# Two DMA rings that cut a batch into windows: equal transfers of 32 KB packets, and thirteen staged batches in place of twelve

## The chip, the cores and the metric

The kernel runs on one core of a Trainium2 chip. Its time is the device time of one execution in microseconds, and the figure that counts is the median over several runs. One more execution was recorded by the hardware profiler, and everything said about stages comes from that execution.

## What is computed

The input `x` has 32 batches of 4096 rows of 256 floats, 4 MiB a batch. The output holds, for each batch, 127 windows of 64 rows, each starting 32 rows after the one before:

```python
for i in range(n_windows):            # (4096 - 64) // 32 + 1 = 127
    start = i * stride                # stride 32, window_size 64
    result[:, i] = x[:, start:start + window_size].copy()
```

There is no arithmetic. With a block of 32 rows (32 KB, 128 blocks to a batch) as the unit, window w consists of blocks w and w+1. A window is 64 KB, and a batch of the output is 127 x 64 KB. Each block but a batch's first and last goes to two places: the second half of one window and the first half of the next.

## The kernel before

All work is done by DMA. Two engines issue it, SyncE (SP) and ScalarE (ACT), and each fills a ring of its own on the core's 16 DMA engines. In the profile SP's ring is q1 and ACT's is q10. A batch takes one of two ways.

**Copied batches** (20, on SP's ring). The windows are copied from HBM to HBM, 127 rows of 64 KB. `copy` makes three transfers of a batch, by `COPY_PARTS`: 80 rows with each row in 4 packets of 16 KB, 32 rows in 2 packets of 32 KB, and 15 rows in 4 packets of 16 KB. The first two are dealt out to 16 DMA engines and the third to 15, so that 15 engines carry 5 + 2 + 1 = 8 rows of a batch and one carries 7.

**Staged batches** (12, the odd ones from 1 to 23, in `STAGED`; on ACT's ring). `load` brings the 128 blocks to one of five SBUF tiles, a block to a partition. `store` writes the tile twice, once to the first halves of the windows and once to the second halves, 128 blocks each time. Each of the three transfers has 16 KB packets (`2 * BLOCK_PARTS` parts of 64 KB), so 16 packets to a DMA engine. ACT issues load n+1 before it waits for load n and issues the two stores of n. The 128th block of a store doesn't belong to the batch: one store runs over into the first half window of the batch above, the other into the last half window of the batch below. What stands there has to be written again.

**The order** (`_order`). A batch beside a staged one is therefore copied after its neighbours' stores have landed, which SP waits for (`after_store`, line 73). Four such batches, `EARLY`, are copied first of all; ACT waits for them (`early`) before the first store that touches them, and at the end SP writes their spoilt half windows again with small transfers of 16 packets of 2 KB (`half`, called the mends here; 7 of them). The other copies are placed in SP's program by a formula that puts each some way behind the stage that it depends on. SP issues all copies one after another with no other waits; the ring itself holds it back when it is full. Last, SP waits for everything and clears the semaphores, one instruction for each.

Of the kernel before, what the change touches and what calls it, by code (L numbers as in the profile page):

```python
# [1 line left out]

# [4 lines left out]


STAGED = tuple(range(1, 24, 2))
BUFS = 5  # L10

EARLY = (18, 20, 22, 24)

BLOCK_PARTS = 2

COPY_PARTS = ((80, 4), (32, 2), (15, 4))


class _Geometry:


    def __init__(self, x, out, W, S):
        self.B, self.L, self.D = x.shape
        self.x, self.out = x, out
        self.n_win = (self.L - W) // S + 1
        self.n_blk = self.L // S
        self.blk = S * self.D
        self.win = W * self.D
        assert W == 2 * S and self.n_blk == self.n_win + 1 == 128

    def src(self, b, block, dims):

        at = (b * self.n_blk + block) * self.blk
        return bass.AP(self.x.tensor, self.x.offset + at, dims)

    def dst(self, b, half, dims):

        at = b * self.n_win * self.win + half * self.blk
        return bass.AP(self.out.tensor, self.out.offset + at, dims)

    def rows(self, b, w0, n):

        s, d = [[self.blk, n], [1, self.win]], [[self.win, n], [1, self.win]]
        return self.dst(b, 2 * w0, d), self.src(b, w0, s)

    def half(self, b, half, block):

        dims = [[self.blk // 16, 16], [1, self.blk // 16]]
        return self.dst(b, half, dims), self.src(b, block, dims)


class _Kernel:
    def __init__(self, nc, g, tiles):
        self.nc, self.g, self.tiles = nc, g, tiles
        self.loaded = [nc.alloc_semaphore(f"loaded{i}") for i in range(len(tiles))]
        self.stored = [nc.alloc_semaphore(f"stored{i}") for i in range(len(tiles))]
        self.copied = nc.alloc_semaphore("copied")
        self.early = nc.alloc_semaphore("early")
        self.count = {}

    def start(self, engine, out, in_, sem, parts=1):
        engine.dma_start(out=out, in_=in_, max_dma_last_dim=65536 // parts).then_inc(sem, 16)
        self.count[id(sem)] = self.count.get(id(sem), 0) + 16

    def all_of(self, engine, sem):
        engine.wait_ge(sem, self.count[id(sem)])

    def slot(self, n):
        return divmod(n, len(self.tiles))

    def after_store(self, engine, n):
        turn, i = self.slot(n)
        engine.wait_ge(self.stored[i], 32 * (turn + 1))

    def load(self, n):

        g, (_, i) = self.g, self.slot(n)
        if n >= len(self.tiles):
            self.after_store(self.nc.scalar, n - len(self.tiles))
        src = g.src(STAGED[n], 0, [[g.blk, g.n_blk], [1, g.blk]])  # L80
        self.start(self.nc.scalar, self.tiles[i][:, :], src, self.loaded[i], 2 * BLOCK_PARTS)

    def store(self, n):

        g, (turn, i) = self.g, self.slot(n)
        self.nc.scalar.wait_ge(self.loaded[i], 16 * (turn + 1))
        for half in (0, -1):
            dst = g.dst(STAGED[n], half, [[g.win, g.n_blk], [1, g.blk]])  # L90
            self.start(self.nc.scalar, dst, self.tiles[i][:, :], self.stored[i], 2 * BLOCK_PARTS)

    def copy(self, b, sem):

        w = 0
        for rows, parts in COPY_PARTS:
            self.start(self.nc.sync, *self.g.rows(b, w, rows), sem, parts)
            w += rows
        assert w == self.g.n_win


def _order(B):


    near = {b for s in STAGED for b in (s - 1, s + 1)}
    order = list(EARLY) + [b for b in range(B) if b not in near and b not in STAGED]
    tied = sorted(near - set(EARLY))
    n = len(order) + len(tied)
    for b in tied:
        behind = max(STAGED.index(s) for s in (b - 1, b + 1) if s in STAGED)  # L110
        order.insert(-(-(2 * behind + 5) * n // (2 * len(STAGED))), b)
    return order


@with_exitstack
def kernel(
    ctx: ExitStack,
    tc: tile.TileContext,
    x: bass.AP,
    window_size: bass.AP,  # L120
    stride: bass.AP,
    out: bass.AP,
):
    nc = tc.nc
    W, S = int(window_size), int(stride)
    g = _Geometry(x, out, W, S)
    assert 0 not in STAGED and g.B - 1 not in STAGED
    pool = ctx.enter_context(tc.tile_pool(name="blocks", bufs=1))
    tiles = [pool.tile([g.n_blk, g.blk], x.dtype, name=f"xb{i}") for i in range(BUFS)]

    with tc.tile_critical():
        k = _Kernel(nc, g, tiles)
        for b in _order(g.B):
            if b not in EARLY:
                for s in (b - 1, b + 1):
                    if s in STAGED:
                        k.after_store(nc.sync, STAGED.index(s))
            k.copy(b, k.early if b in EARLY else k.copied)
        k.load(0)
        waited = False  # L140
        last = len(STAGED) - 1
        for n, s in enumerate(STAGED):
            if n < last:
                k.load(n + 1)
            if not waited and (s - 1 in EARLY or s + 1 in EARLY):
                k.all_of(nc.scalar, k.early)
                waited = True
            k.store(n)


        k.all_of(nc.sync, k.early)
        for n, s in enumerate(STAGED):
            if s - 1 in EARLY or s + 1 in EARLY:
                k.after_store(nc.sync, n)
            if s - 1 in EARLY:
                k.start(nc.sync, *g.half(s - 1, 2 * g.n_win - 1, g.n_blk - 1), k.copied)
            if s + 1 in EARLY:
                k.start(nc.sync, *g.half(s + 1, 0, 0), k.copied)
        for n in range(len(STAGED)):
            k.after_store(nc.sync, n)  # L160
        k.all_of(nc.sync, k.copied)
        for sem in [*k.loaded, *k.stored, k.copied, k.early]:
            nc.sync.sem_clear(sem)


# [1 line left out]
_INS = ['x', 'window_size', 'stride']  # L167
_OUTS = [((32, 127, 64, 256), 'float32')]

_NUMBERS = {'window_size': 64, 'stride': 32}  # L170


# [26 lines left out]
```

## Time and profile before

| what | value |
|---|---|
| median of 3 runs | 767.76 us (767.14 to 767.97) |
| the profiled execution, its own time | 768.4 us |
| the profiled execution, its span | 766.6 us |
| transfers of SP: copies, mends | 60, 7 |
| transfers of ACT: loads, stores | 12, 24 |
| issue to landing, median, 5120 KB copies | 114.8 us |
| issue to landing, median, stores | 84.6 us |
| issue to landing, median, loads | 123.2 us |

The span runs from the program's first instruction to its last. No compute engine does anything but four small memsets, so the only parts of the profile that say something are those on DMA: the busy share of the 16 DMA engines in 40 slices of the span, the rate beneath it, the table of queues, and the same for any stretch that one asks for. A busy share can come out at 1.01 or 1.02 in a short stretch, because a packet is counted where it starts and a packet's record begins slightly before the last one's end.

The long times from issue to landing are times in the ring: a transfer waits there behind those issued before it.

### The profile page before, as it was taken

Reading aid. Unit: us, or ns where it says so; the run is one execution under the profiler, and the core shown is the slowest. Engines: PE = TensorE matmul, PEld = TensorE weight load, DVE = VectorE, ACT = ScalarE, POOL = GpSimd, SP = SyncE. Lnnn points to the kernel's source line nnn. Section 1 sums busy time; section 2 is a strip of 40 time slices with the busy share of each in tenths; the row PEclk is TensorE's granted clock in tenths of the full one; section 3 lists DMA queues with packets and bytes.
Section 4 is the critical chain, followed back from the end, with each engine's and each line's share of the span. In section 5 each row is a group of like instructions: output and inputs, shape, how many; then the busy total and the mean of one; then the engine's idle time right before and its main releaser. Section 6 shows DMA issues by size and latency. Waiting matters only on the chain. (4 is left out here: it accounts for less than half of the span.)

```text
span 766.6 us, 180 instructions
## 1 busy us (share of the span) xinstructions
POOL 0.2 (0%) x4
## 2 busy tenths in 40 slices
POOL 0000000000000000000000000000000000000000
DMA  8999999999999999999999999999999999999996
GB/s 371 425 410 421 405 428 431 408 411 427 423 415 421 431 415 425 432 408 416 427 420 417 431 420 420 423 428 410 414 427 419 422 428 418 417 428 421 420 406 237
DMA packets 19837, 317.70 MB, mean 414 GB/s; under 512 B 1628, under 2 KB 1628, under 8 KB 1740
## 3 DMA queue, kind: packets, MB, share of 16 engines
q1 hardware_dynamic: 10044, 166.70, 51.9%
q10 hardware_dynamic: 9792, 151.00, 47.3%
q14 instruction: 1, 0.01, 0.0%
HBM read 217.02 MB, written 267.35 MB: 632 GB/s over the span
## 5 line engine op out<-in xcount | busy, mean ns | idle before, releaser
L180 POOL MEMSET const-bfloat16-1.0<- 128x1 bf16 x1 | 0.1, 102 | 0.0
L180 POOL MEMSET const-uint8-127<- 128x1 uint8 x1 | 0.1, 102 | 0.0
L180 POOL MEMSET const-float32-0.0<- 128x1 f32 x1 | 0.1, 99 | 0.2 <-issue 0.2
L180 POOL MEMSET const-float32-1.0<- 128x1 f32 x1 | 0.1, 99 | 0.0
## 6 DMA issues: line engine op xcount, KB each, us to landing
out_dram<-in_x_dram SPq DMA_DIRECT2D x20, 5120.0 KB, 114.8
out_dram<-xb ACTq DMA_DIRECT2D x24, 4096.0 KB, 84.6
xb<-in_x_dram ACTq DMA_DIRECT2D x12, 4096.0 KB, 123.2
out_dram<-in_x_dram SPq DMA_DIRECT2D x20, 2048.0 KB, 116.7
out_dram<-in_x_dram SPq DMA_DIRECT2D x20, 960.0 KB, 97.7
out_dram<-in_x_dram SPq DMA_DIRECT2D x7, 32.0 KB, 48.3
```

Of the source, the lines that this page charges most:

```text
L180: nc = _bacc.Bacc("TRN2", target_bir_lowering=False, num_devices=1)
```

## The change

All transfers get packets of 32 KB (`start` has `parts=2` of 64 KB as its default), and all but a few have 8 packets to a DMA engine.

- **Copies.** A batch is copied as windows 0 to 63 and windows 63 to 126, 64 rows each, so window 63 is written twice with the same data. The second half of a batch is issued after the first half has landed (two semaphores, `half`, in turn), and the first half of the next batch is put in the ring before that. The loop `_copies` writes out this order: first half of batch c, wait for the first half of c-1, second half of c-1. One batch, `FIRST` = 28, is cut otherwise: 48 rows at the start of the program, 64 behind them, the last 15 rows at the end of all copies.
- **Staging.** `STAGED` has 13 batches, 1 to 25, so 19 are copied. `EARLY` is 20, 22, 24, 26. A load or a store is one transfer of 8 packets to an engine.
- **The end.** The last staged batch is stored in three parts by `LAST`, 32, 32 and 64 blocks; the first two, at the batch's two edges, have a semaphore of their own (`fringe`), and the last mends wait for that one alone. All semaphores are cleared by one instruction.

The tiles, their number, the order of loads and stores in ACT's program, and the formula for the place of the copies stay as they were.

```diff
-STAGED = tuple(range(1, 24, 2))
+STAGED = tuple(range(1, 26, 2))
 BUFS = 5
-EARLY = (18, 20, 22, 24)
-BLOCK_PARTS = 2
-COPY_PARTS = ((80, 4), (32, 2), (15, 4))
+EARLY = (20, 22, 24, 26)
+FIRST, FIRST_ROWS = 28, 48
+ROWS = 64
+LAST = ((0, 32), (96, 32), (32, 64))
...
-    def start(self, engine, out, in_, sem, parts=1):
+    def start(self, engine, out, in_, sem, parts=2):
...
-        self.start(self.nc.scalar, self.tiles[i][:, :], src, self.loaded[i], 2 * BLOCK_PARTS)
+        self.start(self.nc.scalar, self.tiles[i][:, :], src, self.loaded[i])
...
+    def store(self, n, p0, rows, sem=None):
+        g, (_, i) = self.g, self.slot(n)
         for half in (0, -1):
-            dst = g.dst(STAGED[n], half, [[g.win, g.n_blk], [1, g.blk]])
-            self.start(self.nc.scalar, dst, self.tiles[i][:, :], self.stored[i], 2 * BLOCK_PARTS)
-    def copy(self, b, sem):
-        w = 0
-        for rows, parts in COPY_PARTS:
-            self.start(self.nc.sync, *self.g.rows(b, w, rows), sem, parts)
-            w += rows
+            dst = g.dst(STAGED[n], 2 * p0 + half, [[g.win, rows], [1, g.blk]])
+            self.start(self.nc.scalar, dst, self.tiles[i][p0 : p0 + rows, :], sem or self.stored[i])
+    def copy(self, b, w0, n, sem):
+        self.start(self.nc.sync, *self.g.rows(b, w0, n), sem)
...
+    k.copy(FIRST, 0, FIRST_ROWS, k.copied)
+    k.copy(FIRST, FIRST_ROWS, ROWS, k.copied)
+    for c in range(1, len(order) + 1):
+        if c < len(order):
+            for n in [] if order[c] in EARLY else _beside(order[c]):
+                k.after_store(nc.sync, n)
+            k.copy(order[c], 0, ROWS, sems(c)[0])
+            first_half = k.count[id(sems(c)[0])]
+        if c > 1:
+            nc.sync.wait_ge(sems(c - 1)[0], before)
+            k.copy(order[c - 1], n_win - ROWS, ROWS, sems(c - 1)[1])
+        before = first_half
+    k.copy(FIRST, FIRST_ROWS + ROWS, n_win - FIRST_ROWS - ROWS, k.copied)
...
+        if n < last:
+            k.store(n, 0, g.n_blk)
+        else:
+            for p0, rows in LAST:
+                alone = p0 > 0 and p0 + rows < g.n_blk
+                k.store(n, p0, rows, None if alone else k.fringe)
...
+        if n == len(STAGED) - 1:
+            k.all_of(nc.sync, k.fringe)
+        elif s - 1 in EARLY or s + 1 in EARLY:
+            k.after_store(nc.sync, n)
...
-        for sem in [*k.loaded, *k.stored, k.copied, k.early]:
-            nc.sync.sem_clear(sem)
+    for sem in k.sems:
+        k.all_of(k.nc.sync, sem)
+    k.nc.sync.sem_clear(range(used[0], used[-1] + 1))
```

## The prediction

> **What bounds the kernel now.** I read the page first: the span, the rate in 40 slices, the queues.
>
> ```profile
> span 766.6 us, 180 instructions
> ...
> DMA  8999999999999999999999999999999999999996
> GB/s 371 425 410 421 405 428 431 408 411 427 423 415 421 431 415 425 432 408 416 427 420 417 431 420 420 423 428 410 414 427 419 422 428 418 417 428 421 420 406 237
> DMA packets 19837, 317.70 MB, mean 414 GB/s; under 512 B 1628, under 2 KB 1628, under 8 KB 1740
> ...
> HBM read 217.02 MB, written 267.35 MB: 632 GB/s over the span
> ```
>
> The engines are busy from the first slice to the last but one, so no wait of a sequencer shows: what counts is the bytes that the fullest DMA engine moves, and how long packets take. The rate moves between 405 and 432 GB/s at full busy share, so packets are stretched in some stretches. To find which, I read the timeline for the times at which ACT starts a pair of stores (a load has just landed then), and asked for the rate by stretches: the 25 us before such a time (the load is moving), the stretch after it (the stores), and some picked ones. Columns: stretch, length, memsets, clock, busy share of the DMA engines, GB/s.
>
> ```profile
> 147.00:172.00 25.00, 0.00 (x0) 1.00 0.99 397
> 276.00:301.00 25.00, 0.00 (x0) 1.00 1.02 425
> 524.00:549.00 25.00, 0.00 (x0) 1.00 1.00 406
> ...
> 172.00:212.00 40.00, 0.00 (x0) 1.00 1.01 426
> 301.00:338.00 37.00, 0.00 (x0) 1.00 1.00 427
> 549.00:585.00 36.00, 0.00 (x0) 1.00 1.01 425
> ...
> 312.00:332.00 20.00, 0.00 (x0) 1.00 1.01 433
> 724.00:744.00 20.00, 0.00 (x0) 1.00 0.94 403
> ```
>
> The ten load stretches of loads 2 to 11 run at 397 to 427, mean 414.5; the nine store stretches between them at 422 to 429, mean 425.0; the cleanest stretch at 433. At 724 to 744 the share is 0.94, which is 15/16: the engine that carries 7 rows of each batch has run out of work. The other 15 decide.
>
> **The sum before, for one of those 15.** Copies: 20 batches x 8 rows x 65,536 B = 10.486 MB. Staged: 12 x 24 blocks x 32,768 B = 9.437 MB. Together 19.923 MB. At the clean rate, 433/16 = 27.06 GB/s, that is 736.2 us. The first packets come at about 2.0 us (rate in the first slices of the first 20 us), and the last 2.9 us move nothing (763.7 to 766.6: share 0.00). So 766.6 - 736.2 - 2.0 - 2.9 = **25.5 us are stretched packets and spread between engines**. The stretches place them: a load stretch loses 25 x (1 - 414.5/433) = 1.07 us, a store stretch of 38 us loses 38 x (1 - 425/433) = 0.70 us; twelve of each are 12.8 + 8.4 = 21.2 us. The other 4.3 us fit the end, where the engines finish one after another:
>
> ```profile
> 752.00:754.00 2.00, 0.00 (x0) 1.00 0.97 369
> 754.00:756.00 2.00, 0.00 (x0) 1.00 0.88 328
> 756.00:758.00 2.00, 0.00 (x0) 1.00 0.78 286
> 758.00:760.00 2.00, 0.00 (x0) 1.00 0.74 246
> 760.00:762.00 2.00, 0.00 (x0) 1.00 0.29 110
> 762.00:764.00 2.00, 0.00 (x0) 1.00 0.06 22
> ```
>
> Their idle shares add up to 2 x (0.03 + 0.12 + 0.22 + 0.26 + 0.71 + 0.94) = 4.6 us, less the resting engine's 12/16 = 0.75 us.
>
> **The change, part by part, in the same terms.**
>
> *A batch moves from copied to staged.* Copies: 19 x 524,288 B = 9.961 MB (batch 28, 48 + 64 + 15 rows, makes the same 3 + 4 + 1 rows on 15 engines). Staged: 13 x 786,432 B = 10.224 MB. Together 20.185 MB, or 745.9 us at 27.06 GB/s: **+9.7 us**. A staged batch costs an engine 24 blocks, a copied one 16. HBM itself is not relieved by much: 214 MB read and 269 written, 483 MB after against 484.4.
>
> *One row twice.* The second write of window 63 makes 128 rows of 127. It falls on the sixteenth engine, which rests from before 724 us on: nothing on the other 15. If that engine were as slow as the slowest, it would still only draw level.
>
> *Packets of 32 KB.* The page shows no price of a packet alone. A stretch without 32-row copies (548 to 560 us) ran at 433, one with them (712 to 720) at 437, 0.9%. So the gain lies between 0 and 0.009 x 746 = 6.9 us. The short stretch is blurred by its edges, so I take a value nearer the lower half, **-3.0 us**.
>
> *Clears.* The twelve, 11 of which go, start between 764.9 and 765.6 us:
>
> ```profile
> L163 SPq EVENT_SEMAPHORE_RANGE_CLEAR  x12: 25/30/39, 764.9 to 765.6; - x12
> ```
>
> They follow each other at 0.7/11 = 0.06 us; 11 fewer are 0.7 us, of which I leave 0.1 for the waits that are added beside the one that stays: **-0.6 us**. These lie behind the last landing, so nothing hides them.
>
> *SP's new waits.* SP now waits for the first half of c-1 before it issues its second half; behind that wait stand the first half of c+1, the stores' waits for it, and at the end the mends. SP waited before too:
>
> ```profile
> SPq L62 <- DMA out_dram<-xb: 61.2, 2, 40.2
> SPq L73 <- DMA out_dram<-xb: 19.2, 3, 9.4
> SPq L66 <- DMA out_dram<-in_x_dram: 7.7, 1, 7.7
> ```
>
> Its first 80 us of waiting passed at a share of 1.0, as transfers were queued far ahead (114.8 us median from issue to landing). After the change, when a first half lands, two transfers stay queued, 16 packets. A 32 KB packet takes 32,768/27.06 = 1.21 us, and the rings alternate, so 16 x 2.42 = 39 us of cover for a landing, a wake-up and an issue. The engines' spread of some 10 us (752 to 762) fits in it: **0 us**. With the cover gone the other ring would take the turns, and time would only be lost where that one is dry too; 19 such waits at 1 us (a pair of stores takes 1.0 us of ACT to issue) would be 19 us.
>
> *The last store in three, and the mends.* The mends come behind the edge parts, while the middle part's 8 packets (9.7 us alone) still move. Two mends at 0.5 us of issue (L62's shortest, 510 ns) and the 7.3 us from issue to landing that is the shortest in the trace make 8.3 us and just fit: 0, or up to 8.3 us if that cover is gone.
>
> *Stretched packets.* This is the term that decides. The added load brings its own stretch. What loads lose I keep: 13 x 1.07 = 13.9 us; the ring of ACT still goes from stores to loads and back 13 times, and nothing in the diff touches that. In the store stretches the copies' size changes (4, 2, 4 parts) disappear, and the two rings no longer turn over at different times; what they lose lies between 0 and 0.70 us, and I take half, 13 x 0.35 = 4.6 us. The end, between 2 and 4.3 us, I take at 3.5, as both rings now run out together (304 and 312 packets an engine). Sum **22.0 us** for 25.5.
>
> The Trainium skill has a rule against this change. "DMA: Bandwidth & Descriptors", section "Latency and other measured facts", says that copies between HBM tensors lose rate when the rows of one transfer lie a large power of two apart: 207 GB/s at 512 KiB where 214 is full, and half at 4 MiB. If an engine takes neighbouring rows, 64-row copies put engines 4 x 64 = 256 KiB apart, the old 80-row ones 320 KiB; no view of this run shows how rows are dealt out. Applied to the copies alone, the 3% at 512 KiB would be an estimate of +12 us on top of the sum.
>
> **The forecast.** 2.0 + 745.9 - 3.0 + 2.9 - 0.6 + 22.0 = 769.2 us of span, 2.6 above 766.6. The profiled execution took 768.4 us with its span of 766.6, and the median is 767.76, so a span stands 1.16 us below the median: **770.4 us, slightly slower**. Its own range, from the packet gain (0 to 6.9) and the store stretches (0 to 9.1), is 766 to 777.
>
> **Rivals.**
>
> *Faster.* The stretching is a matter of transfers of different sizes meeting at different times; once all are alike and end in the same turn, load stretches lose it too. For: at 276 to 301 a load runs at 425, and 312 to 332 shows that full rate holds for 20 us on both rings. Against: the load stretches are slow with and without a change of the copies' size in them. Price: loads lose half (7.0), stores nothing, the end 2.0: 9.0 in place of 22.0, span 756.2, **757.4 us**. It decides from where stalls fall below 766.6 - 747.2 = 19.4 us, that is 6.1 less than now.
>
> *Much slower.* Both rings change transfers in the same turn, so that neither covers the other, and all packets run in step. For: the rate at 164 to 168, where the ring of ACT changes from load to stores, is 369, a loss of 4 x (1 - 369/433) = 0.6 us. Against: changes from one store to the next show nothing (312 to 332 has one). If loads run as at 80 to 96 (401 GB/s) throughout and the stores as now: 13 x 25 x 0.074 = 24, 13 x 0.70 = 9, the end 4.3: 37 us, span 784, **786 us**.
>
> *The change doesn't do what it says:* engines drift apart (10 us at the end now, four 32 KB turns), the rings do not turn over together, and the stalls stay at 25.5 + 1.8 for the 13th batch: span 774.5, **775.7 us**.
>
> **How the numbers follow.** Forecast 0.40, faster 0.34, drifting 0.16, much slower 0.10. Runs differ by 0.1%, so 0.2% (1.5 us) is about what can be told from no change. The forecast's own range reaches from 766 to 777, which gives 0.13 to "the same" and 0.03 to faster; with the rival that is faster 0.36, same 0.14, slower 0.50. For 8 in 10 the range takes in most of the faster rival and the drifting one: 757 to 778. The likeliest case's own range is the 766 to 777 above.
>
> **What would show it.** Bytes: 323 MB on the page, q10's share above q1's. Packets of 32 KB alone: a clean stretch above 433 (436 is the -3 us). Load stretches again near 415 and store stretches above 425: the forecast. Load stretches at 425 and more: the faster rival. Rates under 400 at every change of transfer: the slower one. A share below 1.0 in mid-run, with SP waiting for copies: the cover of 39 us was not there. The prediction is wrong if the stalls, 747.2 taken from the new span, lie outside 18 to 30 us.

## The result and the profile after

The changed kernel takes 769.51 us (median of 21 runs, 767.95 to 770.97) against 767.14 us of the kernel before in the same session: ratio 1.003, 95% interval 1.0023 to 1.0036. It is slower by 2.4 us, 0.3%. Of all the runs reported here one, of the kernel with quarters of a load, was in a slower state of the chip and is left out of that kernel's median. The profiled execution's span is 767.1 us, the page's columns are as before:

```profile
span 767.1 us, 157 instructions
...
DMA  9999999999999999999999999999999999999997
GB/s 383 434 413 437 413 432 431 412 429 434 419 424 431 425 419 427 425 420 436 419 420 434 419 422 432 427 417 431 434 408 434 436 407 436 432 408 432 432 425 299
DMA packets 11389, 323.13 MB, mean 421 GB/s; under 512 B 1423, under 2 KB 1423, under 8 KB 1535
...
q10 hardware_dynamic: 5680, 163.58, 50.6%
q1 hardware_dynamic: 5709, 159.55, 48.8%
HBM read 214.07 MB, written 268.60 MB: 629 GB/s over the span
```

The rate over the span rose from 414 to 421 GB/s, so the change did speed transfers up. It spent this on 5.4 MB more bytes. The stretches show where the rate rose. These are four neighbouring ones of the changed kernel, stores, load, stores, load (stretch, length, memsets, clock, busy share, GB/s):

```profile
338.00:374.00 36.00, 0.00 (x0) 1.00 1.00 433
374.00:398.00 24.00, 0.00 (x0) 1.00 1.00 412
398.00:433.00 35.00, 0.00 (x0) 1.00 1.00 433
433.00:457.00 24.00, 0.00 (x0) 1.00 1.00 414
```

Between the landings of loads 2 to 11, all nine store stretches run at 431 to 434 GB/s (mean 432.8; 424.5 for the eight of the kernel before, cut in the same way), all ten load stretches at 412 to 419 (mean 414.5, before 414.7). All store stretches now run at the clean rate, and the load stretches have not moved.

SP now waits most of the time, and the transfer engines are not held up by it:

```profile
SPq L72 <- DMA out_dram<-in_x_dram: 633.4, 18, 56.7
```

The 18 waits for first halves sum to 633 us at a busy share of 1.00.

The end is shorter too. Before, the engines fell idle from 752 us on. After the change they work to 760 us and stop nearly together:

```profile
756.00:758.00 2.00, 0.00 (x0) 1.00 1.00 426
758.00:760.00 2.00, 0.00 (x0) 1.00 1.01 428
760.00:762.00 2.00, 0.00 (x0) 1.00 0.60 254
762.00:764.00 2.00, 0.00 (x0) 1.00 0.21 86
```

### The profile page after: what moved, and what is told of

It reads as the page before. It is cut to its first block, busy times and chain, and to the rows that moved or that the text cites. A ratio compares the mean times of both kernels' runs of the same rounds, so it can differ in the third digit from the quotient of the medians.

```text
span 767.1 us, 157 instructions
## 1 busy us (share of the span) xinstructions
POOL 0.2 (0%) x4
## 2 busy tenths in 40 slices
DMA packets 11389, 323.13 MB, mean 421 GB/s; under 512 B 1423, under 2 KB 1423, under 8 KB 1535
```

## The experiments

Twelve kernels ran. Times are medians; each is compared with the kernel before in its own session (766.3 to 767.0 us), and the changed kernel's 1.003 is the mark to hold them against.

### Twelve staged batches in the changed kernel

```diff
-STAGED = tuple(range(1, 26, 2))
+STAGED = tuple(range(1, 24, 2))
-EARLY = (20, 22, 24, 26)
+EARLY = (18, 20, 22, 24)
```

> The changed kernel with 12 staged batches in place of 13 (EARLY moved down by two), so that each of the 16 DMA engines moves 9.7 us less at 27.06 GB/s, ACT's ring has one load stretch less (1.04 us), and SP's ring has 32 packets more than ACT's (320 to 288), which run alone at the end. Theory 'bytes and load stretches': about 769.5 - 9.7 - 1.0 = 758.8 us, and up to 7 us more if the 32 packets that run alone do so at 366 GB/s, as at the end of the kernel before: 759 to 766 us. Rival 'the rings must run out together' (HBM itself is the bound, and copies alone are slow): 768 to 772 us.

770.22 us, ratio 1.0041 (1.0027 to 1.0056). The 10.7 us that the bytes and one load promised did not come. ACT's ring runs out near 714 us, and copies alone follow for 50 us:

```profile
695.00:710.00 15.00, 0.00 (x0) 1.00 1.01 433
730.00:735.00 5.00, 0.00 (x0) 1.00 0.95 308
735.00:740.00 5.00, 0.00 (x0) 1.00 1.02 334
750.00:755.00 5.00, 0.00 (x0) 1.00 1.02 347
```

At a full busy share the engines move 323 GB/s from 730 to 760 us, where they move 433 beside stores. From 710 to 760 us the mean is 334, and 50 us at 334 instead of 433 lose 50 x (1 - 334/433) = 11.4 us, about what the batch saved. So the thirteenth batch is not why the changed kernel is slower: what it costs in bytes, twelve batches lose at the end.

### Copies at the end on both rings

```diff
+    for w0, rows in ((0, 64), (64, 48), (112, 15)):
+        k.start(nc.scalar, *g.rows(TAIL, w0, rows), k.copied)
```

The twelve-batch kernel, with batch 30 taken from SP's order and issued by ACT last.

> The run with 12 staged batches, but with one of the 20 copies (batch 30) issued by ACT after its last stores, so that both rings have 304 packets an engine and copies run on both at the end instead of on SP's alone. Theory 'copies alone are bound by HBM': the last 40 us still near 320 GB/s, 769 to 771 us. Rival 'a single ring of copies is bound by its own latency': the last 40 us at 430 GB/s, 13 us less than with 12 staged batches, 757 us.

769.41 us, ratio 1.0038 (1.0026 to 1.0051), as with twelve batches:

```profile
735.00:740.00 5.00, 0.00 (x0) 1.00 1.00 321
740.00:745.00 5.00, 0.00 (x0) 1.00 1.03 334
```

Two rings of copies go no faster than one (324 GB/s from 730 to 760 us), so a single ring's latency is not the cause. Nor is each engine's own pace. In the kernel before with 32 KB packets, which comes next but one, copies also run alone at the end, and there the engine with fewer rows has run out of work. Yet 15 engines move the same bytes in the same time as 16. This is q1 from 730 to 760 us, first with twelve staged batches, then in that kernel (packets, MB, share of the engines' time):

```profile
q1 hardware_dynamic: 350, 9.68, 99.7%
q1 hardware_dynamic: 359, 9.86, 93.9%
```

So copies alone meet a limit that the engines share. HBM may be that limit, but its total traffic alone doesn't give the rates. Each byte copied is read from HBM and written to it, so some 320 GB/s on the engines is 640 GB/s at HBM. Beside stores, with half of the bytes copied, the engines' 433 GB/s make 433 x 1.5 = 650 at HBM, and in the slower load stretches 414.5 x 1.5 = 622. No run separates what reads and writes have in it. And the 433 beside stores is not this limit: with loads from SBUF, below, the engines also stop at 433, with far less traffic at HBM.

### Packets of 16 KB

```diff
-    def start(self, engine, out, in_, sem, parts=2):
+    def start(self, engine, out, in_, sem, parts=4):
```

> The changed kernel with packets of 16 KB throughout (all transfers still alike and ending in the same turns). The prediction's term of -3.0 us for packets of 32 KB: 772.5 us. Rival 'a packet's length costs nothing': 769.5 us. Third, 'the packets' length is what keeps the store stretches clean': store stretches back near 425 GB/s, 778 us.

770.5 us, ratio 1.0049 (1.0036 to 1.0062): some 1.1 us more than the changed kernel, by medians (3.5 against 2.4 over the kernel before), between the two expectations. The store stretches run at 430 to 432, mean 431.2, so equal packets of either length keep them clean; 32 KB are worth 0.4% there (432.8 against 431.2), and as much in the load stretches (414.5 against 412.7). From 0 to 690 us this kernel moves 291.51 MB, the changed one 292.49; at 424 GB/s that is 2.3 us.

### The kernel before with 32 KB packets alone

```diff
-BLOCK_PARTS = 2
+BLOCK_PARTS = 1
-COPY_PARTS = ((80, 4), (32, 2), (15, 4))
+COPY_PARTS = ((80, 2), (32, 2), (15, 2))
```

> The kernel before with packets of 32 KB throughout and nothing else changed (80 + 32 + 15 rows, 12 staged). The prediction's term of -3.0 us for the packets: 764 us, and up to 2 us less where the change of packet size between a batch's parts cost something. Rival 'a packet's length costs 1 us at most' (as the changed kernel with 16 KB packets showed): 766 to 767 us.

777.42 us, ratio 1.0139 (1.0124 to 1.0155), slower by 11 us and outside both expectations. The profile tells why. The rings take turns packet by packet: in the kernel before, 272 packets of q1 and 271 of q10 start between 312 and 332 us. In the packet records of the changed kernel from 338 to 374 us, where a single packet starts within 6 ns of another's end, it is of the other ring in 395 of 399 cases. So the packets' sizes divide the engines between the rings. The 16 KB parts of the kernel before gave its rings 560 and 576 packets an engine; with 32 KB throughout they have 320 and 288, and copies run alone from about 708 us on:

```profile
710.00:720.00 10.00, 0.00 (x0) 1.00 0.95 326
```

Against the changed kernel with twelve batches, which has the same packets on both rings, this kernel loses another 8 us (spans 776.1 and 768.1). By 690 us it has moved 291.97 MB against 292.82, which is 2.0 us at 424 GB/s; the other 6 us are lost at the end, where its copies are left alone earlier. So not all of the 8 us can be put down to transfers that end in the same turns.

### The kernel before with 13 batches and 32 KB packets

As above, with `STAGED` to 25 and `EARLY` 20 to 26.

> The kernel before with 13 staged batches and 32 KB packets throughout, its copies still 80 + 32 + 15 rows and no waits: the same packets per engine and ring as the changed kernel (304 and 312), in other transfers. Theory 'transfers that end in the same turns are worth 6 us': 774 to 777 us. Rival 'equal packets and rings that run out together are enough': 769.5 us.

773.74 us, ratio 1.009 (1.0077 to 1.0103). The first theory's time, less 0.3. The packets, the length of both rings and the bytes of 15 engines are as in the changed kernel (the sixteenth has a row a batch less), and other transfers cost 4.7 us more. But most of that is not lost where the theory had it. The store stretches run at 429.4 on average, below the changed kernel's 432.8, and the load stretches at 417.8, above its 414.5, so that by 690 us the kernel has moved 291.78 MB against 292.49, or 1.7 us less. The rest is the end: from 745 us on copies are almost alone (q1 77.0%, q10 19.3% of the engines' time from 745 to 755).

### Rings shifted against each other

```diff
-FIRST, FIRST_ROWS = 28, 48
+FIRST, FIRST_ROWS = 28, 16
-    k.copy(FIRST, FIRST_ROWS + ROWS, n_win - FIRST_ROWS - ROWS, k.copied)
+    k.copy(FIRST, FIRST_ROWS + ROWS, 32, k.copied)
+    k.copy(FIRST, FIRST_ROWS + ROWS + 32, n_win - FIRST_ROWS - ROWS - 32, k.copied)
```

> The changed kernel with batch 28 cut as 16 + 64 + 32 + 15 rows in place of 48 + 64 + 15, so that SP's ring changes transfers 4 packets (9.7 us) away from where ACT's does; nothing else differs. Theory 'alike packets are enough': 769.5 us, store stretches at 433 GB/s. Rival 'ending in the same turns is what cleans the store stretches': store stretches at 425, 13 x 0.70 = 9 us more, 778 us.

774.95 us, ratio 1.0112 (1.0093 to 1.0132). The shift costs 5.6 us, but not where the rival had put it: the store stretches run at 430.0 on average, the load stretches at 411.3 in place of 414.5. Over 35 and 24 us these are 0.23 and 0.19 us, or 5.4 us over 13 batches. By 690 us the kernel has moved 290.95 MB against 292.49, which is 3.6 us. Ending in the same turns matters, and about as much for loads as for stores; only this one shift, of 4 packets, was run.

### Copies in unequal parts, without and with SP's waits

```diff
-            k.copy(order[c - 1], n_win - ROWS, ROWS, sems(c - 1)[1])
+            k.copy(order[c - 1], ROWS, FIRST_ROWS, sems(c - 1)[1])
+            k.copy(order[c - 1], ROWS + FIRST_ROWS, n_win - ROWS - FIRST_ROWS, sems(c - 1)[1])
```

This is the edit of the run with waits; the other leaves out the wait line as well.

> The changed kernel with copies of 64 + 48 + 15 rows, 32 KB packets, no row twice, and so none of SP's waits between a batch's parts; the sixteenth engine has one row a batch less. Theory 'SP's waits cost nothing and hold nothing together': 769.5 us, the store stretches still at 433 GB/s. Rival 'the waits hold the rings in step': store stretches back at 425, 778 us. Rival 'the waits cost something': under 768 us.

> The changed kernel with copies of 64 + 48 + 15 rows as in the run without waits, but with SP's waits of the changed kernel between the 64 rows and the rest. Theory 'SP's waits hold the rings in step': store stretches at 432 GB/s throughout, near 769.5 us. Rival 'unequal transfers and the lighter sixteenth engine are what lets the rings drift': as without the waits, 773 to 775 us.

773.74 us, ratio 1.0095 (1.0078 to 1.0111) without the waits, and 773.2 us, ratio 1.010 (1.0073 to 1.0128) with them. In these kernels the waits neither cost nor help. The parts of 64, 48 and 15 rows cost 4 us, with store stretches at 429.9 and 431.0. By 690 us 1.4 and 2.3 us of it are lost (291.90 and 291.51 MB against 292.49), and the rest at the end, which turns round. This is q1, the copies, and q10 from 755 to 765 us, first in the changed kernel, then in the run without waits (packets, MB, share of the engines' time):

```profile
q10 hardware_dynamic: 110, 2.62, 61.0%
q1 hardware_dynamic: 183, 0.18, 5.1%
```

```profile
q1 hardware_dynamic: 249, 2.98, 76.0%
q10 hardware_dynamic: 18, 0.26, 6.4%
```

The changed kernel ends with stores, which run almost alone at 426 to 428 GB/s (756 to 760 us, above); the others end with copies, which don't. Whether the 15-row part with its resting engine or the unequal parts as such let the rings drift was not separated.

### Loads without HBM

```diff
+        if n > 0:
+            src = self.tiles[4][:, :]
+            self.after_load(self.nc.scalar, 0)
```

> The changed kernel with loads 2 to 13 copied from the tile of the first load instead of from HBM (same transfers, same bytes on each DMA engine, same changes between loads and stores in ACT's ring; the 12 staged batches after the first are left unread and their output is the first one's). Theory 'load stretches are slow because loads and copies both read HBM': the former load stretches run at 430 GB/s and more, about 12 x 1.04 us less, 757 us. Rival 'it is the change between loads and stores, or the writing of SBUF': they stay at 412 to 419 GB/s, 769.5 us.

These are the main lines of the edit. The kernel leaves out the reading of twelve batches: their tiles are filled from the first one's, four tiles serve in turn, and what is stored for them is the first batch's data.

761.07 us in a single run, span 759.0. Load stretches, the loads moving the same bytes on the same engines:

```profile
314.00:338.00 24.00, 0.00 (x0) 1.00 1.01 436
430.00:454.00 24.00, 0.00 (x0) 1.00 1.01 434
```

All ten are at 427 to 437, mean 433.2: as fast as the stores. So it is the loads' reading of HBM, beside copies that read it too, that stretches the load stretches, and not the writing of SBUF or the change of direction in ACT's ring. The same rows bear on the bound: half of the bytes are copies here, so HBM sees about 433 GB/s, and still the mean is no higher than that of the store stretches with their 650. The gain is 8.1 us of span and not the 12.5 expected. By 720 us this kernel has moved 309.63 MB against 305.37, which is 9.8 us at 433 GB/s; at the end it loses some of it again, with 375 GB/s from 731 to 750 us.

### Loads dealt out between the stores

Quarters and eighths of a load, each ahead of two stores of as many blocks (in `_staged`, two batches ahead; `chunk` stores as many blocks to both places), and halves by columns, each ahead of one store. With quarters and eighths the copies that wait for a stage are also placed a little later:

```diff
-            k.store(n, 0, g.n_blk)
+            for j in range(CH):
+                if n + 2 <= last:
+                    k.load(n + 2, j)
+                k.chunk(n, j)
```

> The changed kernel with each load in 4 transfers of 32 blocks (2 packets an engine), each followed in ACT's ring by the two stores of 32 blocks of the batch two stages before it, so that ACT's ring reads HBM in a third of its packets all along and never 8 in a row (copies that depend on a stage stand 12 packets later). Theory 'load stretches are slow because both rings read HBM for 20 us on end': nearly all stretches at 430 GB/s, 13.5 us less at most, 757 to 762 us. Rival 'every change from stores to loads and back costs': four times as many of them at 1.04 us a pair, 13 x 3 x 1.04 = 41 us more, 800 us and over. Third, 'each load packet costs the same wherever it stands': 769.5 us.

> As the run with quarters, but 8 transfers of 16 blocks to a load (1 packet an engine, every eighth block of the batch), each followed by two stores of 16 blocks. Theory 'both rings reading on end': 755 to 760 us, at or under the run with quarters. Rival 'every change costs': twice what the quarters cost, 840 us and over. Third, 'each load packet costs the same': 769.5 us. ACT issues 24 transfers a stage instead of 3, some 10 us of 59.

> The changed kernel with each load in two transfers of all 128 blocks, half of each block (16 KB packets, 8 to an engine), one ahead of each of the two stores: the same 16 engines and 128 partitions as before, twice the changes between loading and storing, half as long each. Theory 'each load packet costs the same wherever it stands': 769.5 to 771 us. Rival 'every change costs': 13 x 1.04 = 13.5 us more, 783 us. Rival 'reading on end costs': 762 to 766 us.

858.59 us, 924.89 us and 803.77 us; ratios 1.1249 (1.1196 to 1.1302), 1.2056 (1.2025 to 1.2088) and 1.0479 (1.046 to 1.0499). All are far slower, in the direction of "every change costs", but two to three times dearer than that rival had it, and at no single price. ACT's ring goes from loads to stores 12 times in the changed kernel. The halves by columns add 12 such changes and 35 us, the quarters 32 and 90 us, the eighths 76 and 156 us, which is 2.9, 2.8 and 2.1 us each. Part of it is that engines no longer end together. With quarters:

```profile
800.00:820.00 20.00, 0.00 (x0) 1.00 0.82 216
820.00:840.00 20.00, 0.00 (x0) 1.00 0.48 159
840.00:856.00 16.00, 0.00 (x0) 1.00 0.10 43
```

Here the engines lose 20 x 0.18 + 20 x 0.52 + 16 x 0.90 = 28 us on average. Why the rest is lost is open: the quarters and eighths also use transfers of 32 and 16 partitions, and the halves other packet sizes, which these runs don't take apart.

## Why the prediction was right

The forecast was 770.4 us, slightly slower, and the measured time is 769.51. The two large terms, bytes and load stretches, were right. That the sum came so near is partly luck. The forecast span was 769.2 us and the measured one is 767.1, so the span was 2.1 us too high. The step from span to median was 1.2 us too low: it took 1.16 us from a profiled execution of the kernel before that was 0.64 us above its median, and here the median stands 2.4 us above the span. Within the span, too, two terms missed in opposite directions.

- **The bytes, +9.7 us for the thirteenth batch: right as a sum, too narrow as a cause.** The page has 323.13 MB and HBM 482.7 MB, as forecast. But twelve batches in the changed kernel are no faster (1.0041). The step took an engine's clean rate of 27.06 GB/s for whatever is in the rings. Copies alone run at about 320 GB/s in all. HBM moved 484.4 MB before and 482.7 after, at 632 and 629 GB/s over the span. That is near the 640 at which copies alone stop, but no run shows that HBM holds back the whole kernel: the store stretches go beyond it, with 650.
- **Load stretches, 13 x 1.07 = 13.9 us kept: right.** They measure 24 x (1 - 414.5/433) = 1.02 us each. The run with loads from SBUF shows the cause.
- **Store stretches, 13 x 0.35 = 4.6 us left: mis-sized.** They lose nothing (432.8 GB/s). The gain comes in steps: 424.5 before, 427.6 with 32 KB packets in the kernel before, 430.0 with all alike but shifted, 432.8 in step. Not all of it is won, though: with 32 KB packets in the old transfers the load stretches ran at 417.4, and in step at 414.5.
- **Packets of 32 KB, -3.0 us: about right in size, taken off the wrong base.** 432.8 against 431.2 GB/s in the store stretches is 0.4%, or 2.8 us of 746; by medians the whole kernel gains about 1.1 us. But the clean rate of 433 that the sum began from is that of 32 KB packets, so the gain had been counted already. The 20 us stretch of 16 KB packets that gave 433 has a busy share of 1.01, which is some 429 at a full share.
- **SP's waits, 0 us: right,** by the busy share of 1.00 and, with unequal copies, by the pair of runs with and without waits.
- **The last store in three, and the mends, 0 to 8.3 us: right but for 0.3 us.** After the last store has landed, SP waits that long for the last mend.
- **The end, 3.5 us: somewhat less.** Idle shares of 0.40 and 0.79 in two stretches of 2 us from 760 on make 2.4 us. That stores and not copies end last is part of it.
- **One row twice, nothing: not measured by itself.** The kernels without it (64 + 48 + 15 rows) are slower, but they differ in more.

Put together with the measured terms: 2.0 + 745.9 + 2.3 for the ends + 13 x 1.02 = 13.3 + 2.4 = 765.9 us, of a span of 767.1; 1.2 us stay unplaced. Against the kernel before, in the same terms, the span gains 0.5 us: 9.7 for the bytes and 0.5 for one more load stretch are added, and 1.2 unplaced; 8.4 for the store stretches, 1.9 at the end and, by the forecast, 0.6 for the clears are taken off.

The rivals: the faster one fails where it was aimed, at the load stretches (412 to 419, as before). Its other terms, no loss in store stretches and 2.0 us at the end, came nearly true (0 and 2.4), and the stalls, 767.1 - 747.2 = 19.9 us, lie only 0.5 us above the 19.4 that was its border. The much slower one fails: no stretch of the changed kernel between two loads is under 431, so both rings changing in the same turn leave no gap; the shifted run shows the opposite. As for drifting engines: the kernels with unequal copies take 773 to 774 us, near that rival's 775.7, but no view shows single engines, so whether they drift there is open. The rule on rows a large power of two apart, from the Trainium skill's "DMA: Bandwidth & Descriptors", section "Latency and other measured facts", finds no support here. With 64-row copies the store stretches run at as high a steady rate as in any of these runs, and copies alone run at 323 GB/s in 64 rows and at 329 in 80, 32 and 15. How rows are dealt to engines no run showed.

## What to carry to other kernels

Here the two DMA rings took turns on the same engines packet by packet, so packet sizes decide how the rings share the engines and which one is left alone at the end; make that the one that runs well alone (here stores, 426 to 428 GB/s, and not HBM-to-HBM copies, about 320). A rate that is measured with both rings busy may not be carried over to a stretch in which only one kind of transfer is left. Kernels with the same packets in other transfers took 4 to 8 us more of some 770, of which 1.4 to 3.6 us had gone by 690 us and the rest went at the end. The thirteenth staged batch by itself neither won nor lost: 770.22 us without it, 769.51 with it.

## What the hardware showed that was not expected

- HBM-to-HBM copies alone reach about 320 GB/s, 640 GB/s read and written, on one ring or two and on 15 engines as on 16; beside stores from SBUF the same engines move 433. The Trainium skill's "HBM Reference", section "Specifications (TRN2)", gives 716 GB/s for the memory that two cores share; the most that a stretch makes here is the 650 worked out for copies beside stores.
- Loads beside copies run at 414 GB/s where they read HBM, and at 433 where the same bytes come from SBUF.
- Splitting the loads into parts among the stores cost 35 to 156 us, far more than the 13 us that all load stretches lose.
- Changing only the packets' size in the kernel before, from 16 to 32 KB, made it 11 us slower.
